# State space outputs through DRAM: the projection of a hybrid decoder step moved out of the chunk scan into three dense passes

## The chip, the cores and the metric

One Trainium2 chip, one core of it. The metric is the device time of one execution in microseconds (us), as the median of several runs. Five engines work beside each other: PE (TensorE, matmuls; its weight loads are listed as PEld), DVE (VectorE), ACT (ScalarE), POOL (GpSimd) and SP (SyncE, which here issues every DMA). Matmul results land in PSUM banks, everything else lies in SBUF or in DRAM.

## What is computed

One layer of a hybrid decoder step, for 1024 prompt tokens and 8 single-token samples that share the weights (1032 columns in all, D = 1024). A modulated RMSNorm feeds one input projection `h @ w_in`, whose columns are q, k, v of 12 attention heads, the state space streams z, xBC and dt, and two branch gates. Then, for each of 8 state space groups (256 channels each):

```
y   = scan(conv(xBC), dt) + d_skip * x         # chunks of 128 tokens, one state per head
y   = y * silu(z)
y   = y * rsqrt(mean(y*y over the group) + eps) * norm_g
```

and for the layer

```
merged = sigmoid(g_a) * (attn @ w_o_attn) + sigmoid(g_s) * (y @ w_o_ssd)     # y has 2048 channels
x      = x + g1 * (merged @ w_out)
x      = x + g2 * (relu(norm(x) @ w_up)**2 @ w_down)
```

All of it in float32 accuracy: each operand of a matmul is split into a rounded part and a remainder (hi, lo), and a product is three matmuls, hi·hi, hi·lo and lo·hi.

## The kernel before

**Layout.** Activations lie transposed: 128 channels on the partitions, the 1032 tokens along the row, in three column chunks of 384, 384 and 264 (`CH`).

**Dense jobs.** `Dense` (line 101) makes 128 output channels. It loads its weights through `load_raw` (SP), casts them on ACT (`whi`, line 97) and subtracts on POOL (`wlo`, line 98). Then, per column chunk, it accumulates 3 matmuls for each of 8 input tiles (lines 142 to 144) into one of three PSUM banks `mm` and calls an evacuation. A step is such a column chunk: 24 matmuls with 8 input tiles, 12 with 4, 6 with 2. `run` (line 181) loads the weights of the next job ahead, and after each step advances `clock` by one and lets the side work go on by `pace` items (`pump`, line 158).

**Side work.** Generators in `sides` yield between items. `rest(n)` makes one wait for n steps, so that the dense matmuls of those steps stand between two items on PE. The order on PE is that in which the program is written; on the other engines a planner orders the instructions. While `gated[0]` is set, a step whose activations find too few free `ck` buffers (19 of 384 columns and 10 of 264, counted in `live`) first drains side items two at a time (line 134).

**The scan stage.** The main jobs are z (2 jobs) and x/B/C (4 jobs, with the convolution in their evacuation, line 798) of each group. Beside them run, per group (`ssd_sides`, line 815): `chunks` (line 1002; 8 chunks, each `prep`, `state`, `out`; `prep` is called two chunks ahead), `decode` (line 824; the samples' states) and `finish_` (line 1034). `finish_` takes each column chunk through `sums` (product with the gate z on POOL, squares), `rstd` (a reciprocal root in ten small DVE instructions on 3 columns) and `norm` (three transposes on PE that spread the root, the scaling at line 969, hi on ACT, lo on POOL). Then it calls `project` (line 976):

```
for f in range(8):                       # 128 output channels each
    for ci, (t0, nt) in enumerate(CH):
        ps = ps_mm()
        for t in range(2):               # 2 tiles x 3 matmuls, lines 991 to 993
            ...
        V.tensor_tensor(sacc[f][:, t0:t0 + nt], ps[:, :nt], sacc[f][:, t0:t0 + nt], op=OP.add)   # 997
```

So each group adds its share of `y @ w_o_ssd` to eight accumulators in SBUF (`sacc`), 24 times 6 matmuls.

**After the scan.** Eight jobs for the attention gate (`ga_job`, line 1160), eight for the state space gate (`gs_job`, line 1166) with the merge of the three attention groups beside them (`merge`, line 1192), eight for the attention's output projection (`oa_job`, line 1243; only 2 input tiles, so 6 matmuls a step, and a chain of DVE, POOL, ACT and DVE behind each), then `w_out` (`wo_job`, line 1264), norm and MLP.

Of the kernel before, what the change touches and what calls it, by code (L numbers as in the profile page):

```python
# [19 lines left out]
NT = S + NB  # L20
# [20 lines left out]
def _trunk(ctx, tc, nc, I, O):  # L41
# [42 lines left out]
    def load_w(src, r0, kt, c0, n, side=False, into=None, raw=None):  # L84
# [3 lines left out]
        if into:  # L88
            hi, lo = into
        elif side:  # L90
            hi = wp.tile([128, 256], F32R, name="shi", tag="shi", bufs=2)
            lo = wp.tile([128, 256], F32R, name="slo", tag="slo", bufs=2)
# [8 lines left out]
    class Dense:  # L101

        def __init__(self, src, r0, c0, n, x, evac, pre=None, halo=0):
            self.a = (src, r0, c0, n, x, evac, pre)
            self.halo = halo
            self.units = self.raw = None

        def fetch(self, kt=4):
            if self.raw is None:
                src, r0, c0, n, x, *_ = self.a  # L110
                nk = self.nk = len(x[0]) if isinstance(x, tuple) else 8
# [101 lines left out]
    dsel = consts.tile([128, 16, 17], F32, name="dsel")  # L213

# [5 lines left out]
    ac_d = dram.tile([2, 32, 1024], F32, name="ac_d")  # L220

# [53 lines left out]
    def rstd_cols(sq, scale, eps, pool):  # L275

        ps = ps_()
        for i in range(3):
            T.matmul(ps[:, i:i + 1], sq[:, i * 128:(i + 1) * 128], ones, start=True, stop=True)
        r = pool.tile([128, 3, 3], F32, name="rstd", tag="rstd", bufs=2)  # L280
        V.tensor_scalar(r[:, 1], ps[:, :3], scale, eps, op0=OP.mult, op1=OP.add)
# [465 lines left out]
    sacc = []  # L747

    def acc_tiles():
        return [accp.tile([128, NT], F32, name="acc", tag="acc", bufs=8) for _ in range(8)]  # L750
# [64 lines left out]
    def ssd_sides(gi, tl):  # L815
# [8 lines left out]
        def decode():  # L824
# [13 lines left out]
            def load(bh):  # L838
# [37 lines left out]
        def load(c):  # L876
# [3 lines left out]
            ar = D_[c] = sd.tile([128, 4, 128], F32, name="ar", tag="ar", bufs=3)  # L880
            dma(ar, dap(ac_d, 4 * gi * 1024 + c * 128, [[0, 128], [1024, 4], [1, 128]]))

        def prep(c):
            ar = D_.pop(c)
            er = None
            if c:
                er = sd.tile([128, 2, 128], F32, name="er", tag="er", bufs=2)
# [59 lines left out]
        sq_, rs_, hi_, lo_ = {}, {}, {}, {}  # L947

        def sums(ci):
            nt = CH[ci][1]  # L950
# [603 lines left out]
```

## Time and profile before

| | |
|---|---|
| runs, us | 2492.43 median; 2486.13 to 2492.50 (3 runs) |
| the profiled execution, us | 2494.12; its span from first to last instruction 2492.3 |
| PE busy | 2357.0 us, 95% of the span, 15243 matmuls and transposes |
| DVE, ACT, POOL busy | 51%, 35%, 30% |
| TensorE clock granted, mean | 0.98 of full speed |
| DMA | 254.75 MB, 16 engines 35% busy |

Matmuls are pipelined, so "busy" covers small losses: how long matmuls take is read better from how many of them a stretch holds. A wait is listed with what ended it. In the listing of waits the columns are the total in us, the number of times and the longest.

### The profile page before, as it was taken

Reading aid. Unit: us, or ns where it says so; the run is one execution under the profiler, and the core shown is the slowest. Engines: PE = TensorE matmul, PEld = TensorE weight load, DVE = VectorE, ACT = ScalarE, POOL = GpSimd, SP = SyncE. Lnnn points to the kernel's source line nnn. Section 1 sums busy time; section 2 is a strip of 40 time slices with the busy share of each in tenths; the row PEclk is TensorE's granted clock in tenths of the full one; section 3 lists DMA queues with packets and bytes.
Section 4 is the critical chain, followed back from the end, with each engine's and each line's share of the span. In section 5 each row is a group of like instructions: output and inputs, shape, how many; then the busy total and the mean of one; then the engine's idle time right before and its main releaser. Section 6 shows DMA issues by size and latency. Waiting matters only on the chain.

```text
span 2492.3 us, 40904 instructions
## 1 busy us (share of the span) xinstructions
PE 2357.0 (95%) x15243; PEld 2240.5 (90%) x15243; DVE 1264.3 (51%) x3520; ACT 863.1 (35%) x2162; POOL 738.7 (30%) x702
## 2 busy tenths in 40 slices
PE   4999999999999999999999999989999999999998
PEld 2878898988999999989898999989999999999997
DVE  4443233577576768676767434345533333333336
ACT  4333333355543444434343312224321221221232
POOL 1011121244343434434343433343222222222230
PEclk7999999999999999999999999999999999999999
DMA  8254433343433333332333223122544544411111
GB/s 282 82 184 142 149 88 87 102 117 82 103 83 88 90 81 104 78 102 71 100 75 96 61 60 76 51 88 58 174 135 136 174 139 144 146 45 51 55 40 69
DMA packets 332481, 254.75 MB, mean 102 GB/s; under 512 B 21510, under 2 KB 323129, under 8 KB 326506
## 3 DMA queue, kind: packets, MB, share of 16 engines
q1 hardware_dynamic: 332282, 252.14, 34.9%
q8 instruction: 120, 1.97, 0.3%
q14 instruction: 79, 0.65, 0.1%
HBM read 224.50 MB, written 71.81 MB: 119 GB/s over the span
## 4 chain that ended last, share of the span: by engine, by line
PE 53%; DVE 10%; DMA 7%; POOL 3%; issue 3%; ACT 3%; SPq 0%; DVEq 0%; POOLq 0%; ACTq 0%
PE mm L142 16%; PE mm L143 16%; PE mm L144 16%; DMA ar<-ac_d 3%; DVE ck L798 2%; POOL wlo L98 1%; DMA hst<-state_ssm 1%; DVE hst L863 1%; DVE acc L997 1%; DMA bc<-bc_d 1%; ACT ar L907 1%; DMA ssm_sample<-hst 1%; PE ps L935 1%; PE mm L991 1%; PE mm L993 1%
## 5 line engine op out<-in xcount | busy, mean ns | idle before, releaser
L142 PE MATMUL mm<-hh,whi 128*128 128x384 f32 (+3 forms) x2808 | 917.8, 327 | 4.5 <-DVE ck L798 4.5
L144 PE MATMUL mm<-hh,wlo 128*128 128x384 f32 (+3 forms) x2808 | 900.4, 321 | 0.0
L143 PE MATMUL mm<-hl,whi 128*128 128x384 f32 (+3 forms) x2808 | 899.7, 320 | 0.1
L98 POOL TENSOR_TENSOR wlo<-wraw,whi 128x512 fp32r<-128x512 f32 (+1 forms) x300 | 388.4, 1300 | 973.0 <-ACT whi L97 930.9
L142 PEld LDWEIGHTS mm<-hh,whi 128*128 128x128 f32 x2808 | 532.8, 190 | 10.7 <-issue 6.7
L143 PEld LDWEIGHTS mm<-hl,whi 128*128 128x128 f32 x2808 | 532.1, 190 | 0.7 <-DVE hl L1324 0.3
L144 PEld LDWEIGHTS mm<-hh,wlo 128*128 128x128 f32 x2808 | 531.1, 189 | 0.0
L97 ACT CAST whi<-wraw 128x512 fp32r<-128x512 f32 (+1 forms) x300 | 181.8, 612 | 384.5 <-PE mm L143 325.4
L1257 DVE SCALAR_TENSOR_TENSOR acc<-mm,mod,acc 128x384 f32<-128x384 f32 (+1 forms) x216 | 123.6, 573 | 235.3 <-PE mm L144 234.4
L143 PE MATMUL mm<-dl,whi 128*128 128x384 f32 (+1 forms) x696 | 223.3, 321 | 0.0
L144 PE MATMUL mm<-dh,wlo 128*128 128x384 f32 (+1 forms) x696 | 222.3, 319 | 0.0
L142 PE MATMUL mm<-dh,whi 128*128 128x384 f32 (+1 forms) x696 | 222.3, 319 | 0.0
L798 DVE SCALAR_TENSOR_TENSOR ck<-mm,cwT,ck 128x384 f32<-128x384 f32 (+4 forms) x288 | 163.1, 568 | 69.5 <-ACT ck L794 65.8
L1344 DVE TENSOR_TENSOR r<-r 128x384 f32<-128x384 f32 (+1 forms) x96 | 70.0, 729 | 186.3 <-ACT r L1343 186.3
L991 PE MATMUL mm<-ck,shi 128*128 128x384 f32 (+1 forms) x384 | 129.8, 338 | 22.3 <-DVE acc L997 18.4
L910 POOL TENSOR_TENSOR ar<-ar,cb 128x512 f32<-128x512 f32 x64 | 83.2, 1300 | 163.1 <-DVE cb L905 129.6
L142 PEld LDWEIGHTS mm<-dh,whi 128*128 128x128 f32 x696 | 131.1, 188 | 0.0
L143 PEld LDWEIGHTS mm<-dl,whi 128*128 128x128 f32 x696 | 130.9, 188 | 0.0
L144 PEld LDWEIGHTS mm<-dh,wlo 128*128 128x128 f32 x696 | 130.8, 188 | 0.0
L993 PE MATMUL mm<-ck,slo 128*128 128x384 f32 (+1 forms) x384 | 124.5, 324 | 0.5 <-POOL slo L98 0.4
L992 PE MATMUL mm<-ck,shi 128*128 128x384 f32 (+1 forms) x384 | 124.0, 323 | 0.4 <-POOL ck L974 0.4
L907 ACT ACTIVATE ar<-ar,acs 128x128 f32<-128x128 f32 x256 | 85.4, 391 | 109.3 <-DMA ar<-ac_d 109.3
(334 smaller groups left out, 3404.0 us busy)
## 6 DMA issues: line engine op xcount, KB each, us to landing
wraw<-w_in SPq DMA_DIRECT2D x164, 256.0 KB
kv_g_sample<-cache_kv_g SPq DMA_DIRECT2D x144, 256.0 KB
wada<-w_ada SPq DMA_DIRECT2D x24, 1024.0 KB
ar<-ac_d SPq DMA_DIRECT2D x64, 256.0 KB
wraw<-w_up SPq DMA_DIRECT2D x64, 256.0 KB
wraw<-w_down SPq DMA_DIRECT2D x58, 256.0 KB
hst<-state_ssm SPq DMA_DIRECT2D x64, 128.0 KB
bc<-bc_d SPq DMA_DIRECT2D x32, 256.0 KB
```

Source lines behind the costliest of these rows:

```text
L97: A.copy(hi, raw)
L98: P.tensor_tensor(lo, raw, hi, op=OP.subtract)
L142: T.matmul(ps[:n, :m], wh, a, start=(k == 0), stop=False)
L143: T.matmul(ps[:n, :m], wh, b, start=False, stop=False)
L144: T.matmul(ps[:n, :m], wl, a, start=False, stop=(k == nk - 1))
L798: V.scalar_tensor_tensor(acc[:, o:n], ps[:, x0 + o - d:x0 + n - d], w[k], acc[:, o:n], op0=OP.mult, op1=OP.add)
L907: A.activation(ar[:, h, :], ar[:, h, :], AF.Relu, bias=acs[:, c, 4 * gi + h:4 * gi + h + 1], scale=-1.0)
L910: P.tensor_tensor(ar, ar, cb[:, None, :].to_broadcast([128, 4, 128]), op=OP.mult)
L991: T.matmul(ps[:, :nt], hi[:, t, :], a, start=(t == 0), stop=False)
L992: T.matmul(ps[:, :nt], hi[:, t, :], b, start=False, stop=False)
L993: T.matmul(ps[:, :nt], lo[:, t, :], a, start=False, stop=(t == 1))
L1257: V.scalar_tensor_tensor(x[:, t0:t0 + n], ps[:, :n], gate[:, 0:1], x[:, t0:t0 + n], op0=OP.mult, op1=OP.add)
```

## The change

The projection leaves the scan. In the scan a group's gated output `y` is written to DRAM (`y_d`) without its norm, and only the sums of squares are kept (`ysum`). The sixteen gate jobs write the tanh of their results to DRAM (`tg_d`): five stand between the x and B/C jobs of the groups 1 to 5, six behind the last z job, five after the scan. After the scan `yprep` reads `y` back in four quarters of four tiles, normalises it and splits it (hi on ACT, lo now on DVE). `y @ w_o_ssd` becomes three passes of eight dense jobs, with 4, 4 and 8 input tiles; the jobs of the last pass alternate with those of the attention's output projection. The scan's buffers get deeper, and `prep` runs three chunks ahead.

```diff
+    ysum = consts.tile([128, 8, 9], F32, name="ysum")
+    y_d = dram.tile([16, 128, NT], F32, name="y_d")
+    tg_d = dram.tile([16, 128, NT], F32, name="tg_d")
...
-                    hst = sd.tile([128, 2, 128], F32, name="hst", tag="hst", bufs=3)
+                    hst = sd.tile([128, 2, 128], F32, name="hst", tag="hst", bufs=4)
...
-            ar = D_[c] = sd.tile([128, 4, 128], F32, name="ar", tag="ar", bufs=3)
+            ar = D_[c] = sd.tile([128, 4, 128], F32, name="ar", tag="ar", bufs=5)
...
-            xd = sd.tile([128, 4, 64], F32, name="xd", tag="xd", bufs=2)
-            xw = sd.tile([128, 4, 64], F32, name="xw", tag="xw", bufs=2)
-            bt = sd.tile([128, 128], F32, name="bt", tag="bt", bufs=2)
-            cb = sd.tile([128, 128], F32, name="cb", tag="cb", bufs=1)
+            xd = sd.tile([128, 4, 64], F32, name="xd", tag="xd", bufs=4)
+            xw = sd.tile([128, 4, 64], F32, name="xw", tag="xw", bufs=4)
+            bt = sd.tile([128, 128], F32, name="bt", tag="bt", bufs=4)
+            cb = sd.tile([128, 128], F32, name="cb", tag="cb", bufs=2)
...
+        def gate(ci):
+            t0, nt = CH[ci]
             sq = sq_[ci] = [sd.tile([128, 384], F32, name="sq", tag="sq", bufs=2) for _ in range(2)]
             for t in range(2):
                 P.tensor_tensor(X[t][ci][:, :nt], X[t][ci][:, :nt], Z[t][ci][:, :nt], op=OP.mult)
+                dma(y_d[2 * gi + t, :, t0:t0 + nt], X[t][ci][:, :nt])
                 A.activation(sq[t][:, :nt], X[t][ci][:, :nt], AF.Square)
...
-        def rstd(ci):
...
-        def norm(ci):
...
-        def project():
...
+            live[ci // 2] -= 4
+
+        def sums(ci):
+            V.tensor_copy(ysum[:, gi, 3 * ci:3 * ci + 3], col_sums(sq_[ci][0]))
...
             prep(0)
             yield
             prep(1)
-            yield from rest(2)
+            yield from rest(1)
+            prep(2)
+            yield from rest(1)
             for c in range(8):
                 state(c)
                 yield
                 out(c)
-                if c + 2 < 8:
-                    prep(c + 2)
-                load(c + 3)
+                if c + 3 < 8:
+                    prep(c + 3)
+                load(c + 4)
...
+                gate(ci)
+                yield from rest(2)
                 sums(ci)
-                yield from rest(2)
-                rstd(ci)
-                yield from rest(2)
-                norm(ci)
                 yield
-            yield from project()
...
+    def gate_job(i, f, pool, bufs):
+        def ev(ci, t0, nt, ps):
+            t = pool.tile([128, 384], F32, name="tg", tag="tg", bufs=bufs)
+            A.activation(t[:, :nt], ps[:, :nt], AF.Tanh, scale=0.5)
+            dma(tg_d[8 * i + f, :, t0:t0 + nt], t[:, :nt])
+        return Dense(w_in, 0, (GA_C, GS_C)[i] + f * 128, 128, h_, ev)
...
-            main = main + x_jobs(gi + 1, tls[gi + 1])
+            xj = x_jobs(gi + 1, tls[gi + 1])
+            if gi < 5:
+                xj.insert(2, gate_job(*gates.pop(0), sa, 3))
+            main = main + xj
         sides.extend(ssd_sides(gi, tls[gi]))
+    main = main + [gate_job(*gates.pop(0), sa, 3) for _ in range(6)]
     run(main, pace=4.0)
...
+    def yprep(q, tiles):
...
+        r = mg.tile([128, 3, 18], F32, name="yr", tag="yr", bufs=2)
+        V.tensor_scalar(r[:, 1], ysum[:, 2 * q:2 * q + 2, :].rearrange("p g c -> p (g c)"), 1.0 / 256, 4 * EPS,
+                        op0=OP.mult, op1=OP.add)
+        rsqrt_cols(r[:, 0], r[:, 1], r[:, 2])
+        parts = [(g, ci) for ci in range(3) for g in range(2)]
...
+                    y = tg()
+                    dma(y[:, :nt], y_d[4 * q + 2 * g + t, :, t0:t0 + nt])
...
+        load(0)
+        load(1)
+        yield from rest(1)
+        for i, (g, ci) in enumerate(parts):
+            nt = CH[ci][1]
+            ps = ps_()
+            for k in range(3):
+                c = 9 * g + 3 * ci + k
+                T.transpose(ps[:, k * 128:(k + 1) * 128], r[:, 0, c:c + 1].to_broadcast([128, 128]), ident)
+            for t in range(2):
+                y = st[i][t]
+                c = R_SG + 4 * q + 2 * g + t
+                V.scalar_tensor_tensor(y, y, vecT[:, c:c + 1], ps[:, :nt], op0=OP.mult, op1=OP.mult)
+                hi, lo = (x[2 * g + t][ci] for x in yx[q])
+                A.copy(hi, y)
+                V.tensor_tensor(lo, y, hi, op=OP.subtract)
+            load(i + 2)
+            yield from rest(1)
...
+    def os_job(q, f):
+        def ev(ci, t0, nt, ps):
+            if q == 0:
+                A.copy(sacc[f][ci], ps[:, :nt])
+            elif q == 1:
+                V.tensor_tensor(sacc[f][ci], ps[:, :nt], sacc[f][ci], op=OP.add)
+            else:
+                t = ts[f, ci] = tg()[:, :nt]
+                g = tg()[:, :nt]
+                dma(g, tg_d[8 + f, :, t0:t0 + nt])
+                V.tensor_tensor(t, ps[:, :nt], sacc[f][ci], op=OP.add)
+                V.scalar_tensor_tensor(t, g, 1.0, t, op0=OP.add, op1=OP.mult)
...
+    preps = [yprep(q, x) for q, x in enumerate((yt_tiles, hl_tiles, ac_tiles, yt_tiles))]
+    mgs = merge()
+    sides.extend([preps[0], mgs])
+    os_ = [[os_job(q, f) for f in range(8)] for q in range(3)]
+    run([gate_job(*g, gt, GTB) for g in gates], after=os_[0][0], pace=3.0)
+    finish([preps[0], mgs])
...
+    sides.extend(preps[1:3])
+    run(os_[0], after=os_[1][0], pace=1.0)
+    finish([preps[1]])
+    sides.append(preps[3])
+    run(os_[1], after=os_[2][0], pace=1.0)
+    finish(preps[2:])
...
+    run([j for f in range(8) for j in (os_[2][f], oa_job(f))], after=wo[0])
     x1 = acc_tiles()
+    for f in range(8):
+        dma(x1[f], xT_d[f])
...
+    for f in range(4, 8):
+        wo[f].load(into=[tuple(wx.tile([128, 512], F32R, name="wx", tag="wx", bufs=16) for _ in range(2))
+                         for _ in range(2)])
```

`tg()` gives a tile of 384 columns from nine buffers, `ps_()` one of five PSUM banks. The side items of `yprep` and of the merge advance by at most one each per step.

## Rows read from the trace of the kernel before

**Rows 1.** Busy time per stretch: us, each engine's busy us (instructions), clock, DMA share, GB/s

```profile
core 0: us, PE busy (x) PEld busy (x) DVE busy (x) ACT busy (x) POOL busy (x), PEclk, DMA share, GB/s
1800.00:2300.00 500.00, 500.00 (x3183) 500.00 (x3182) 168.88 (x358) 108.19 (x211) 112.16 (x87) 1.00 0.38 120
...
490.00:1460.00 970.00, 923.28 (x6073) 877.28 (x6072) 658.27 (x1945) 418.86 (x1086) 385.89 (x381) 0.99 0.34 89
```

**Rows 2.** The same view for the eight project blocks: first, last, sum

```profile
611.30:638.00 26.70, 25.18 (x147) 24.70 (x146) 15.62 (x67) 18.50 (x53) 8.08 (x10) 0.92 0.56 158
...
1445.30:1473.60 28.30, 24.53 (x148) 22.94 (x147) 19.69 (x56) 4.56 (x13) 13.19 (x19) 1.00 0.36 95
sum 223.50, PE 200.28 PEld 185.51 DVE 178.90 ACT 82.75 POOL 71.48; mean PE 25.03 PEld 23.19 DVE 22.36 ACT 10.34 POOL 8.94
```

**Rows 3.** Instructions of line 991: durations ns, first and last start; waits until

```profile
L991 PE MATMUL mm<-ck,shi x384: 279/334/882, 611.3 to 1473.2; 128*128 128x384 f32 x128, 128*128 128x264 f32 x64
...
  DVE acc L997: 30.5, 42
```

**Rows 4.** Waits of PE over the whole span

```profile
PE mm L142 <- DVE ck L1247: 10.3, 6, 2.4
PE ps L966 <- DVE rstd L233: 8.0, 6, 4.0
...
PE ps L935 <- POOL ar L910: 6.7, 4, 2.2
```

**Rows 5.** Waits of PE from 490 to 1460 us

```profile
PE ps L931 <- DVE state L922: 4.5, 4, 1.8
```

**Rows 6.** Instructions that use the merged attention (tile ath): the projection's first matmuls

```profile
L142 PE MATMUL mm<-ath,whi x48: 282/338/687, 1605.3 to 1642.5; 128*128 128x384 f32 x32, 128*128 128x264 f32 x16
```

**Rows 7.** Busy time per stretch: group 2's scan beside z jobs, beside x jobs, group 0

```profile
757.00:787.00 30.00, 30.00 (x212) 28.30 (x211) 12.88 (x34) 9.99 (x26) 10.96 (x11) 1.00 0.31 78
787.00:833.00 46.00, 43.02 (x278) 41.59 (x277) 37.43 (x96) 24.07 (x59) 20.19 (x19) 0.96 0.27 68
...
523.00:548.00 25.00, 19.70 (x127) 17.14 (x127) 22.24 (x64) 12.63 (x33) 11.53 (x11) 0.92 0.50 134
```

**Rows 8.** DVE instructions by shape, 490 to 1660 us: busy us, mean ns, idle before

```profile
L997 DVE TENSOR_TENSOR acc<-mm,acc 128x384 f32<-128x384 f32 x112 | 61.5, 550 | 6.3 <-PE mm L993 6.2
...
L969 DVE SCALAR_TENSOR_TENSOR ck<-ck,vecT,ps 128x384 f32<-128x384 f32 x32 | 18.8, 605 | 8.4 <-PE ps L966 8.4
...
L969 DVE SCALAR_TENSOR_TENSOR ck<-ck,vecT,ps 128x264 f32<-128x264 f32 x16 | 7.7, 486 | 18.3 <-PE ps L966 18.3
```

**Rows 9.** DVE instructions by shape, 1475 to 1660 us

```profile
L1250 DVE TENSOR_TENSOR hl<-acc,hh 128x384 fp32r<-128x384 f32 x16 | 12.9, 809 | 7.0 <-ACT hh L1249 7.0
...
L1171 DVE SCALAR_TENSOR_TENSOR acc<-ck,acc 128x264 f32<-128x264 f32 x8 | 7.2, 904 | 14.3 <-ACT ck L1169 14.3
L1250 DVE TENSOR_TENSOR hl<-acc,hh 128x264 fp32r<-128x264 f32 x8 | 5.5, 687 | 7.2 <-ACT hh L1249 7.1
...
L1219 DVE TENSOR_TENSOR m<-m 128x256 f32<-128x256 f32 x5 | 4.1, 819 | 5.3 <-POOL m L1218 5.3
```

**Rows 10.** ACT instructions by shape, 490 to 1660 us

```profile
L1249 ACT CAST hh<-acc 128x384 fp32r<-128x384 f32 x16 | 8.2, 514 | 16.4 <-POOL acc L1248 16.4
```

**Rows 11.** POOL instructions by shape, 490 to 1460 us

```profile
L98 POOL TENSOR_TENSOR wlo<-wraw,whi 128x512 fp32r<-128x512 f32 x98 | 130.5, 1338 | 93.7 <-ACT whi L97 87.2 <-PE mm L143 5.6 <-PE mm L144 0.8
```

**Rows 12.** Busy time per stretch: gate jobs with the merge, the attention's projection

```profile
1475.00:1600.00 125.00, 120.67 (x766) 119.44 (x765) 35.83 (x100) 29.10 (x75) 36.19 (x38) 1.00 0.22 54
1605.00:1650.00 45.00, 34.59 (x188) 32.41 (x188) 29.44 (x50) 15.52 (x34) 35.00 (x34) 0.92 0.43 132
```

**Rows 13.** Waits of the DMA queue (SP), 490 to 1800 us

```profile
SPq L81 <- POOL wlo L98: 452.0, 130, 17.2
...
SPq L889 <- DVE xd L900: 62.4, 13, 8.1
```

**Rows 14.** Instructions of line 81 on SP, 490 to 1660 us: ns to issue one

```profile
L81 SPq DMA_DIRECT2D wraw<-w_o_ssd x64: 367/373/458, 596.2 to 1459.7; - x64
```

More of the change, by code (lines that the diff above doesn't have):

```diff
@@ L82, in load_raw, with load_w @@
         return raw
-    def load_w(src, r0, kt, c0, n, side=False, into=None, raw=None):
+    def load_w(src, r0, kt, c0, n, into=None, raw=None):
         if raw is None:
@@ L273, in steps, with col_sums @@
             yield
-    def rstd_cols(sq, scale, eps, pool):
+    def col_sums(sq):
         ps = ps_()
@@ L746, in _trunk, with acc_tiles @@
     sd = None
-    sacc = []
-    def acc_tiles():
-        return [accp.tile([128, NT], F32, name="acc", tag="acc", bufs=8) for _ in range(8)]
+    def acc_tiles(dt=F32):
+        return [accp.tile([128, NT], dt, name="acc", tag="acc", bufs=8) for _ in range(8)]
     def z_jobs(gi, tl):
@@ L1004, in chunks @@
                 yield 'wait'
-            for c in range(3):
+            for c in range(4):
                 load(c)
@@ L1144, in _trunk @@
     sd = sd_cm.__enter__()
-    accp = ctx.enter_context(tc.tile_pool(name="accp", bufs=1, side="right"))
-    sacc.extend(acc_tiles())
+    def gate_job(i, f, pool, bufs):
[4 more added lines that the diff above has]
+        return Dense(w_in, 0, (GA_C, GS_C)[i] + f * 128, 128, h_, ev)
+    gates = [(i, f) for i in range(2) for f in range(8)]
     main = zj0
@@ L1275, in wo_job @@
         return Dense(w_out, 0, f * 128, 128, lambda: g_, ev)
-    def xT_side():
-        for f in range(8):
-            while len(oa_done) <= f:
-                yield 'wait'
-            yield from rest(1)
-            dma(x1[f], xT_d[f])
-            yield
-    sides.append(merge())
-    oa = [oa_job(f) for f in range(8)]
-    mgs = list(sides)[-1]
-    run(gs, pace=3.0)
-    finish([mgs])
-    g_ = h_tiles()
-    x1 = acc_tiles()
-    oa_done = []
-    wo = [wo_job(f) for f in range(8)]
-    sides.append(xT_side())
-    run(oa, pace=0.7, after=wo[0])
-    drain()
+    ts = {}
+    preps = [yprep(q, x) for q, x in enumerate((yt_tiles, hl_tiles, ac_tiles, yt_tiles))]
[4 more added lines that the diff above has]
+    finish([preps[0], mgs])
+    mm_cm.__exit__(None, None, None)
+    accp = ctx.enter_context(tc.tile_pool(name="accp", bufs=1, side="right"))
+    sacc = [[hp_.tile([128, nt], F32, name="sacc", tag=f"hh{ci}", bufs=8) for ci, (_, nt) in enumerate(CH)]
+            for _ in range(8)]
+    sides.extend(preps[1:3])
[4 more added lines that the diff above has]
+    finish(preps[2:])
+    g_ = tuple([[] for _ in range(8)] for _ in range(2))
+    wo = [wo_job(f) for f in range(8)]
+    run([j for f in range(8) for j in (os_[2][f], oa_job(f))], after=wo[0])
+    x1 = acc_tiles()
+    for f in range(8):
+        dma(x1[f], xT_d[f])
+    yt_cm.__exit__(None, None, None)
+    mg_cm.__exit__(None, None, None)
+    wx_cm = tc.tile_pool(name="wx", bufs=1)
+    wx = wx_cm.__enter__()
     n2_cm = tc.tile_pool(name="n2", bufs=1, side="right")
```

143 lines of the change are left out of this document (61 added, 82 removed).

## The prediction

> **What bounds the kernel now.** I read the busy times by stretch first. In the MLP PE works without a gap: 500 us hold 3183 matmuls, so one costs 500/3183 = 0.1571 us on the mean of the three column chunks, at full clock [rows 1]. That is the price of a dense matmul when nothing disturbs it. In the scan PE is named busy for 923 of 970 us, DVE for 658 [rows 1], and still no single engine is full: PE executes in written order, so it loses time wherever a side item is not ready. Next I looked for the stretches that hold too few matmuls. The eight blocks of `project` are such: each has 144 matmuls with nothing dense between them, and together they last 223.5 us [rows 2], where 8 × 144 × 0.1571 = 181.0 us would do. The reason stands in the waits of line 991: the PSUM bank is not free because line 997, the addition to `sacc`, has not run [rows 3]. A step there has only 6 matmuls (0.94 us) per addition of 0.55 us [rows 8], and DVE does the samples' states in the same stretch; it is busy for 178.9 of the 223.5 us [rows 2]. Then I read the waits of PE over the whole span [rows 4]: the reciprocal root ahead of `norm` (8.0 us), the decay matrix of `prep` from POOL (6.7 us) and the attention's projection (10.3 us), which also has 6 matmuls a step and a chain over four engines behind each.
>
> **The change part by part.** The matmuls stay the same in number: 1152 for `w_o_ssd` before, 8 × 3 × (12 + 12 + 24) = 1152 after; 72 transposes for the root before, 4 × 18 after. So PE's own work is not shortened, and all that can be won is lost time.
>
> *Removed.* (1) Dense passes give 12 or 24 matmuls per evacuation, 1.9 or 3.8 us against 0.55, or 2 × 0.55 in the third: 223.5 − 181.0 = **42.5 us**. (2) The attention's projection runs from 1605.3 to its last step at 1642.5 us [rows 6]: 37.2 us for 23 steps, whose 138 matmuls need 21.7; **15.5 us**. Between the jobs of the third pass, each 72 × 0.1571 = 11.3 us, its chain has room. (3) The root leaves the scan, **8.0 us**. (4) `prep` one chunk earlier gives POOL a further step of about 4 us, and the longest such wait is 2.2 us: **6.7 us** [rows 4]. Sum 72.7.
>
> *Added: yprep.* A tile of 384 columns costs DVE 0.605 to scale and 0.809 to subtract, one of 264 columns 0.486 and 0.687 [rows 8, 9]; a part (two tiles) 2.83 or 2.35 us, a quarter 4 × 2.83 + 2 × 2.35 = 16.0 us. Nothing reads these subtractions at once, but PE stands behind the scalings, since each part's transposes need one of five PSUM banks. In the first pass two quarters are due together, two parts per step of 12 × 0.1571 = 1.88 us. The twelfth part can only be transposed when the seventh has been scaled: 3.8 us (two steps) + 7 × 2.83 = 23.6, while PE without waits is there after 7 × 1.88 = 13.2. I take **10.4 us**. Bounds: 0, if the planner scales all parts ahead of the subtractions; 18 us if DVE also waits for the cast of 0.514 us on ACT [rows 10] in each tile (a part is then 3.9 us). In the second pass one quarter is due, and DVE has 2.83 + 0.55 per step, against 1.88, for six steps: 9 us behind, of which three banks `mm` cover some 6; **4 us**, bounds 0 and 12. With the last five gate jobs the first quarter stands beside the merge. Of the 35.8 us of DVE there before [rows 12], some 16 were line 1171 (16 × 0.552 us and 8 × 0.904 [rows 9]); the other 20 belong to five of nine merge items (line 1219 ran five times in it [rows 9]), so 4 us each. Per step that is 2.83 + 4 = 6.8 us against 3.8, for six steps 18 us behind, of which the three buffers of the merge cover about three steps; **5 us**, bounds 0 and 13.
>
> One rule speaks against moving the subtraction from POOL to DVE. The 0.809 us [rows 9] were measured while POOL was busy for 35.0 of 45 us [rows 12], so the disturbance by POOL is in them, and I add nothing. The Trainium skill ("SBUF — State Buffer", section "Who interferes with whom") says that a DVE instruction with two SBUF inputs and a GpSimd instruction that reads SBUF exclude each other, the later one waiting for the whole of the other. By that rule the eight `wlo` casts of the first pass, 1.338 us each [rows 11], could push DVE back by up to 10.7 us more, and the sum would come out that much later.
>
> *Added: DMA.* `y` and the gates make 4 × 8.45 MB (16 tiles of 128 × 1032 × 4 bytes, each written and read), 33.8 MB. At 120 GB/s for a share of 0.38 [rows 1] full use is about 316 GB/s (an estimate), so 107 us of all engines, spread over 1100 us in which a third of them is used. 192 issues at 0.37 us [rows 14] are 71 us of SP; its main wait is for raw weight buffers, 452 us [rows 13], so it has the room. What SP is moved past: each `y` store waits for POOL's product and each gate store for ACT's tanh, and the weight loads written behind them stand still meanwhile. The nearest such wait of the queue is 62.4 us in 13 times, 4.8 each [rows 13]; a job lasts 11.3 us and its weights are asked for a job ahead, so it is hidden. Cost 0, up to 4.8 us for every third of the 24 pairs of stores if a second wait comes on top (38 us).
>
> *Added: x1 and w_out.* The eight loads of x, 4.2 MB, can start only when the third pass has read the tiles that lay there; they take 4.2/0.316 = 13.4 us, beside `w_out`'s weights. The first evacuation comes 6.6 us later (2.8 us of attention steps, 3.8 of the first job). **3 us**, bounds 0 and 14.
>
> *Added: the scan without its project blocks.* In each block DVE did some 11 us of work besides its 24 additions (178.9/8 less 16 × 0.55 + 8 × 0.42). That goes beside z and x jobs. Beside z jobs DVE has room: 12.9 of 30 us busy; beside x jobs it is at 37.4 of 46 [rows 7], but 24 roots and scalings go from there. **4 us**, bounds −10 (the waits of the first group [rows 5] and their clock go too, thanks to deeper buffers) and 35.
>
> *Sum:* added 10.4 + 4 + 5 + 3 + 4 = 26.4. The profiled execution took 2494.1 (span 2492.3); 2494.1 − 72.7 + 26.4 = 2447.8. The median is 1.7 lower: **2446 us**.
>
> **Rivals.**
> *Little is given back.* The planner spreads yprep, and the deeper buffers end the first group's waits: 72.7 + 8 off, 2494.1 − 80.7 + 6 − 1.7 = 2418. For it: DVE is a third full after the scan [rows 1, 12]. Chance 0.15.
> *The preparation becomes the bound.* The three places of yprep and the entry to `w_out` at their upper bounds, 18 + 12 + 13 + 14 + 4 = 61: 2481. For it: DVE waits for ACT's cast behind most of line 1250 [rows 9]; against: the planner has other work to put in. 0.09.
> *The queue takes it back.* SP's stores hold up weights at the worst bound, 38 us beside the 26: 2484 or a little more, so no change. Against: 452 us of slack [rows 13]. 0.06.
> *Slower: the scan loses its cover.* From 523 to 548 us, with no project block in between, PE is busy for 19.7 of 25 us at clock 0.92 [rows 7], DVE for 22.2; it waits for line 922 [rows 5]. If the 11 us of DVE work that each block hid come onto PE's path in all eight groups, 88 us, the time is 2446 + 84 = 2530. It decides when the loss exceeds (72.7 − 22.4)/8 = 6.3 us per group. Against: the room beside z jobs [rows 7]. 0.05.
>
> **How the numbers follow.** The forecast has the remaining 0.65. Its own range is 2428 to 2466. The range for 8 in 10 reaches from 2416 (the better case) to 2482 (the preparation); outside stand the queue, the slower case and what is better still, some 0.18. A measurement of this kernel can tell about 0.3%, 7.5 us, from no change. Faster than 2485: forecast, better case and the preparation, 0.89; within: the queue, 0.06; slower: 0.05.
>
> **What would show it.** Right: the blocks of 6 matmuls are gone; no wait for lines 997, 233 and 1247 of before is left in PE's list; the three passes hold near 1/0.1571 matmuls per us except in the first seven steps of the first pass, where PE waits some 10 us for the scalings; each scan group shrinks by about 29 us, less the 11 of a gate job. Wrong: waits of PE for the state addition or the convolution in every group; PE waiting for casts whose weights landed late behind a store; or passes that run without a wait.

## The result: slower, where a gain was forecast

The changed kernel takes **2521.0 us** (median of 4 runs, 2507.2 to 2525.7), the kernel before 2490.0 (4 runs beside them, 2486.1 to 2492.5): ratio 1.0106, 95% interval 1.0086 to 1.0125. The ratio with its interval is the better measure: the two medians alone give 1.0125, so a difference taken between medians can be off by some 5 us. The forecast was 2446, its range 2416 to 2482. The profiled execution took 2519.6 us, its span is 2517.8.

The page's first row, and PE's waits over the whole span of the changed kernel (us in total, times, longest us), which answer to [rows 4, 5]. In the changed kernel line 926 is the state addition, 935 the matmul that reads the state of the chunk before, 920 the matmul that makes a state, 867 the update of a sample's state, 911 the first pass of the scalar engine over a decay tile `ar`.

```profile
PE 2366.4 (94%) x15243; PEld 2255.6 (90%) x15243; DVE 1200.8 (48%) x3252; ACT 867.0 (34%) x2126; POOL 682.8 (27%) x618
```
```profile
PE ps L935 <- DVE state L926: 30.2, 11, 5.4
...
PE mm L140 <- DVE tg L1287: 14.8, 8, 2.5
PE ps L935 <- ACT ar L913: 13.0, 6, 3.9
...
PE ps L935 <- ACT ar L911: 6.9, 6, 2.0
PE mm L140 <- DVE ysum L966: 6.0, 6, 1.0
```

The waits that were to go are gone: none for the project blocks' additions, the scan's reciprocal root, or the attention's projection of before. In their place PE waits for the state addition, 30.2 us where [rows 5] had 4.5, for the decay tiles, and in pass 3 eight times for line 1287, the attention's gate product.

Busy time by stretch of the changed kernel (us, each engine's busy us and instructions, granted clock, DMA share, GB/s): passes 1 to 3, then the scan, which answers to the second row of [rows 1].

```profile
1441.00:1494.00 53.00, 50.05 (x329) 49.18 (x329) 26.53 (x59) 25.27 (x56) 11.57 (x9) 1.00 0.53 160
1494.00:1541.00 47.00, 47.00 (x307) 46.83 (x306) 23.29 (x47) 10.67 (x21) 9.77 (x8) 1.00 0.18 53
1541.00:1672.00 131.00, 116.15 (x727) 114.70 (x726) 54.19 (x94) 24.07 (x46) 49.25 (x47) 1.00 0.37 116
490.00:1382.00 892.00, 830.85 (x5414) 791.88 (x5414) 528.33 (x1539) 389.72 (x987) 312.45 (x289) 0.96 0.42 109
```

Passes 1 and 2 run as dense work should. Pass 3 loses some 15 us, and the scan's mean clock is 0.96 where [rows 1] had 0.99.

From the first matmul of a state to the last, the scan took 891.8 us before and 804.5 after. By the prediction's own terms it should take 891.8 − 195.2 (seven of the eight blocks lie between, 223.5 − 28.3 [rows 2]) − 8.0 − 6.7 + 56.5 (five gate jobs of 11.3) + 4 = 742. It is 62 too long, and since the 4 are in the sum, the scan's own term came out at 66. Pass 3 with the attention's projection lasts 128.0 to its last job's matmuls; eight pairs of 14.1 (90 matmuls) need 113. These two excesses, 62 and 15, and 5.6 us in the first 510 us, where both kernels are the same, are 83; the span exceeds the forecast by 72, so 11 less must lie elsewhere (a remainder, not measured by itself).

One group shows what happened. Instructions of two lines in group 2 (durations ns min/median/max, first and last start): first before, where line 916 makes the states and line 863 updates the samples, then after.

```profile
L916 PE MATMUL ps<-xw,bt x16: 377/378/462, 726.3 to 797.0; 128*128 128x256 f32 x16
...
L863 DVE SCALAR_TENSOR_TENSOR hst<-hst,dsel,tmp x16: 341/345/1125, 732.5 to 755.3; 128x128 f32<-128x128 f32 x16
```
```profile
L920 PE MATMUL ps<-xw,bt x16: 377/378/463, 733.9 to 788.0; 128*128 128x256 f32 x16
...
L867 DVE SCALAR_TENSOR_TENSOR hst<-hst,dsel,tmp x16: 337/350/1389, 740.7 to 770.1; 128x128 f32<-128x128 f32 x16
```

The samples' update follows 6 to 7 us behind the first state in both. In that time before, no further state was made: in the stretch from 732 to 756 us line 916 has no instruction at all, because PE was in the project block (727.9 to 756.9). After, ten of the sixteen matmuls of line 920 lie between 740 and 771 us, beside the z jobs, whose last evacuation starts at 762.7. The chunks' chain now runs through the samples' update.

What such a meeting looks like, on DVE, then on ACT (start us, us, instruction, and in brackets the idle time before it and what ended it):

```profile
638.01 0.16 DVE L863 TENSOR_TENSOR dx<-ck,dsel 128x2 f32<-128x2 f32 x1
641.18 0.64 DVE L867 SCALAR_TENSOR_TENSOR hst<-hst,dsel,tmp 128x128 f32<-128x128 f32 x2 [3.01 <-ACT tmp L866]
641.74 0.42 DVE L926 TENSOR_TENSOR state<-ps,state 128x256 f32<-128x256 f32 x1
```
```profile
638.91 1.28 ACT L911 ACTIVATE ar<-ar,acs 128x128 f32<-128x128 f32 x4 [4.41 <-DMA ar<-ac_d]
640.22 0.63 ACT L913 ACTIVATE ar<-ar 128x512 f32<-128x512 f32 x1
640.76 0.68 ACT L866 ACTIVATE tmp<-bc,dx 128x128 f32<-128x128 f32 x2
```

ACT stands 4.4 us for a decay tile; the samples' product (line 866) is queued behind it; DVE stands 3.0 us for that product, and the state addition is queued behind the samples' update. PE waits 4.6 us for the addition. In these rows each engine takes up the next instruction only behind the late one, so one late load passes through three engines. The load itself stands on SP behind two stores of the samples' states:

```profile
626.73 4.47 SPq L871 DMA_DIRECT2D ssm_sample<-hst  x2
...
632.31 0.46 SPq L885 DMA_DIRECT2D ar<-ac_d  x1
```

### The profile page after: what moved, and what is told of

Read it like the earlier page. It is cut to its first block, busy times and chain, and to the rows that moved or that the text cites. A ratio compares the mean times of both kernels' runs of the same rounds, so it can differ in the third digit from the quotient of the medians.

```text
span 2517.8 us, 40894 instructions
## 1 busy us (share of the span) xinstructions
PE 2366.4 (94%) x15243; PEld 2255.6 (90%) x15243; DVE 1200.8 (48%) x3252; ACT 867.0 (34%) x2126; POOL 682.8 (27%) x618
## 4 chain that ended last, share of the span: by engine, by line
PE 57%; DMA 9%; DVE 6%; ACT 3%; issue 3%; POOL 2%; SPq 1%; DVEq 0%; ACTq 0%; POOLq 0%
PE mm L140 18%; PE mm L141 18%; PE mm L142 18%; DMA ar<-ac_d 7%; ACT ar L911 2%; DMA tg<-tg_d 1%; DVE ck L802 1%; POOL wlo L95 1%; POOL ck L957 1%; PE ps L939 1%; PE ps L935 0%; DVE hst L867 0%; POOL ar L914 0%; ACT ck L798 0%; DMA ssm_sample<-hst 0%
## 5 line engine op out<-in xcount | busy, mean ns | idle before, releaser
L95 POOL TENSOR_TENSOR wlo<-wraw,whi 128x512 fp32r<-128x512 f32 (+1 forms) x332 | 424.9, 1285 | 1176.0 <-ACT whi L94 1116.6
L140 PEld LDWEIGHTS mm<-hh,whi 128*128 128x128 f32 x2808 | 538.3, 192 | 17.3 <-issue 16.4
L141 PEld LDWEIGHTS mm<-hl,whi 128*128 128x128 f32 x2808 | 537.9, 192 | 0.5 <-DVE hl L1373 0.3
L94 ACT CAST whi<-wraw 128x512 fp32r<-128x512 f32 (+1 forms) x332 | 201.9, 613 | 490.3 <-PE mm L141 416.7
L1392 ACT ACTIVATE r<-mm 128x384 f32<-128x384 f32 (+1 forms) x96 | 43.8, 456 | 153.5 <-PE mm L142 152.9
L867 DVE SCALAR_TENSOR_TENSOR hst<-hst,dsel,tmp 128x128 f32<-128x128 f32 x128 | 60.9, 488 | 68.0 <-ACT tmp L866 67.5
L935 PEld LDWEIGHTS ps<-ck,state 128*128 128x128 f32 x224 | 33.4, 202 | 63.3 <-ACT tmp L866 27.7
## 6 DMA issues: line engine op xcount, KB each, us to landing
hst<-state_ssm SPq DMA_DIRECT2D x64, 128.0 KB
```

Source lines behind the costliest of these rows:

```text
L94: A.copy(hi, raw)
L95: P.tensor_tensor(lo, raw, hi, op=OP.subtract)
L140: T.matmul(ps[:n, :m], wh, a, start=(k == 0), stop=False)
L141: T.matmul(ps[:n, :m], wh, b, start=False, stop=False)
L867: V.scalar_tensor_tensor(hst[:, i, :], hst[:, i, :], ds[:, 8 + 2 * bh + i:9 + 2 * bh + i], tmp, op0=OP.mult, op1=OP.add)
L1392: A.activation(r[:, :nt], ps[:, :nt], AF.Relu)
```

## The experiments

**Buffers and look-ahead as before** (the change's edits to `bufs` and to `chunks` undone):

```diff
-            ar = D_[c] = sd.tile([128, 4, 128], F32, name="ar", tag="ar", bufs=5)
+            ar = D_[c] = sd.tile([128, 4, 128], F32, name="ar", tag="ar", bufs=3)
...
-                if c + 3 < 8:
-                    prep(c + 3)
+                if c + 2 < 8:
+                    prep(c + 2)
```

> The changed kernel (2521.0) with the buffers and the look-ahead of the kernel before: three ar tiles, two of xd, xw, bt and er, one cb, three hst, chunks prepared two ahead. Theory A (the scan pays because nothing lies between a chunk's state and the next chunk any more, whatever the buffers): 2515 to 2540, the same or a little worse. Theory B (the deeper buffers let the planner put work of later chunks and of the samples ahead of the state addition on the vector and scalar engines): 2450 to 2490, with the waits for the state addition (30.2 us on line 926 in the changed kernel) under 10.

2505.6 us, ratio to before 1.0074 (1.0052 to 1.0096): 15 us better, and the state waits are 36.5 us in 28 times. So the depth costs something, but the wait is there without it; neither theory's time was met.

**The state one chunk earlier:**

```diff
+            state(0)
             for c in range(8):
-                state(c)
+                if c < 7:
+                    state(c + 1)
                 yield
                 out(c)
```

> The changed kernel with each chunk's state computed one chunk earlier, so that the output of chunk c finds the state of chunk c-1 a whole chunk old; four state tiles in place of three. Nothing else moves. Theory A (the state addition comes late on the vector engine by a few us, seven times a group, and TensorE waits for it and then runs at half clock): the 30.2 us of waits on line 926 go to under 8, with the half-clock stretches behind them, and the time falls by 30 to 60, to 2460 to 2490. Theory C (the waits are of the scalar engine for the decay tile's load, which come late in any order): TensorE waits for ar in place of the state, and the time stays over 2505.

2488.7 us, ratio 0.9999 (0.9988 to 1.001): 32 us back (27 by the ratios), the scan 771.8, at the upper end of what theory A gave. What is left are mostly waits for `xw` (27.0 us in 8 times) and for a PSUM bank that a late state addition holds (13.8 in 10).

**The samples' states left out**, in the changed kernel and in the one before:

```diff
-            load(0)
-            yield from rest(2)
-            for bh in range(4):
+            for bh in range(0):
```

> The changed kernel without the loop over the samples' states (their loads, update, outputs and stores are left out, so the samples' rows of the scan lack the state term). Theory A (the samples' update collides with the chunks' chain on the vector and scalar engines, now that no projection block gives it a stretch of its own): the lost time of the scan falls by 40 to 70, to 2450 to 2480. Theory D (the collisions are with the convolution's evacuations and weight casts, not the samples): a fall of under 20, 2501 to 2521.

> The kernel before (2490.0) without the same loop over the samples' states. Theory A: the samples' update lay under the projection blocks, where TensorE needed nothing of the state's chain, so little is gained: 2475 to 2490. Theory D, and any theory in which the samples cost the same in both kernels: a fall as large as that of the changed kernel without the loop.

After: 2438.0 us, ratio 0.9798 (0.9783 to 0.9812), the scan 721.0. Before: 2453.6, ratio 0.9862 (0.9847 to 0.9877). The samples cost 83 us after and 37 before (77 and 34 by the ratios); without them the change gains 15.6 us. In the changed kernel that is more than the 40 to 70 of theory A. For the kernel before neither theory was met: the samples were not nearly free there, as theory A had it, and the fall is not as large as after, as theory D had it. In the scan of the changed kernel without samples PE waits for no state and no decay tile; its waits, and its stretch from the first state to the last:

```profile
PE mm L140 <- DVE ysum L964: 4.6, 5, 1.0
PE mm L140 <- DVE ck L802: 3.6, 4, 1.3
```
```profile
509.60:1230.60 721.00, 712.83 (x4873) 687.04 (x4873) 391.60 (x943) 320.89 (x789) 284.77 (x262) 1.00 0.33 86
```

That accounts for the 83: with the samples PE waits 57.8 us in this stretch at a mean clock of 0.96, without them 8.2 us at 1.00. So 50 us are waits, and up to 32 (0.04 of 804.5 us, an estimate) are the lower clock. ACT still stands 95.8 us for decay tiles without the samples, and 111.6 with them:

```profile
ACT ar L909 <- DMA ar<-ac_d: 95.8, 30, 5.2
```
```profile
ACT ar L911 <- DMA ar<-ac_d: 111.6, 43, 5.1
```

So late loads alone hold up nothing on PE in that run; together with the samples they do. The kernel before shows where most of its 37 us lay: the eight project blocks without samples, the sum of their windows beside the sum of [rows 2], and PE's wait for the blocks' additions (line 995 there):

```profile
sum 196.20, PE 187.82 PEld 183.30 DVE 100.59 ACT 49.28 POOL 70.17; mean PE 23.48 PEld 22.91 DVE 12.57 ACT 6.16 POOL 8.77
```
```profile
PE mm L989 <- DVE acc L995: 2.1, 2, 1.2
```

The blocks shrink from 223.5 to 196.2 us. Of the 42.5 us that I had put down to six matmuls per addition, 27 were the samples' work.

The next three each take one link out of the chain. **The product on DVE** (`V.tensor_scalar` for `A.mul`), **the new stores on ACT's queue** (those of `y`, shown below, and those of the gates), and **decay tiles and gate tanh loaded from ACT's queue**:

```diff
-                        A.mul(tmp, bc[:, 0, i, :], dx[:, i:i + 1])
+                        V.tensor_scalar(tmp, bc[:, 0, i, :], dx[:, i:i + 1], None, op0=OP.mult)
```

> The changed kernel (2521.0) with the samples' product tmp (128 products of 128x128) computed on the vector engine in place of the scalar engine. The samples' whole loop cost 83 us in the changed kernel and 37 in the kernel before. Theory A (the vector engine stands 67.5 us in the scan for this product, which lies on the scalar engine behind the decay tiles' wait for their load, and the state addition is queued behind it): the wait goes, and the time falls by 30 to 55, to 2466 to 2491, though the vector engine has some 35 us more to do. Theory E (the cost is the samples' work itself on a vector engine that has to do it ahead of the state addition): no fall, 2515 to 2540.

2515.9 us, ratio 1.0105 (1.0083 to 1.0126), as theory E had it. The wait for ACT is gone by construction, and PE's for the state grew to 50.8 us in 25 times. DVE has 31 us more to do in this run, so it does not tell how much the wait for `tmp` cost; but taking that wait out is not enough, and the samples' work in front of the addition delays it too.

```diff
-                dma(y_d[2 * gi + t, :, t0:t0 + nt], X[t][ci][:, :nt])
                 A.activation(sq[t][:, :nt], X[t][ci][:, :nt], AF.Square)
+                nc.scalar.dma_start(y_d[2 * gi + t, :, t0:t0 + nt], X[t][ci][:, :nt])
```

> The changed kernel with the stores that the change added to the scan (gated outputs to y_d, gate tanh to tg_d) issued by the scalar engine's queue, each right behind a scalar instruction that needs the same data, in place of SP's queue. Theory B (these stores hold SP's queue 83.6 and 30.2 us while they wait for their data, and make the decay tiles' loads late, for which the scalar engine waits 113 us in all): the scalar engine's wait for ar falls below 60 and the time by 25 to 50, to 2470 to 2496. Theory A (the stores are not the cause; the scalar engine waited 109 us for ar in the kernel before too): within 10 us of 2521.

2502.6 us, ratio 1.0041 (1.0023 to 1.0059); ACT's wait for `ar` fell from 111.6 to 84.7 in the scan, which is 787.5. PE's own waits for decay tiles (13.0 and 6.9 us) are gone from its list, while those for the state are 39.2. Between the two theories: the stores, costed at nothing, do cost something like 18 us (16 by the ratios).

```diff
-            dma(ar, dap(ac_d, 4 * gi * 1024 + c * 128, [[0, 128], [1024, 4], [1, 128]]))
+            nc.scalar.dma_start(ar, dap(ac_d, 4 * gi * 1024 + c * 128, [[0, 128], [1024, 4], [1, 128]]))
```

> The changed kernel with the decay tiles' loads in the scan, and the gate loads in the third pass, issued by the scalar engine's queue. In the scan, theory C (the late load of ar is the first cause: no lateness, no wait for tmp behind it): the scalar engine's wait for ar falls from 113 to under 40 and the scan's stretch from the first state to the last from 804 to 760 to 780. Against it: the scan stays over 795. In the third pass, if the gate loads are late because they stand behind weight loads in SP's queue, the eight waits of about 1.9 us for line 1287 go, and the stretch of pass 3 with the attention's projection shrinks from 128 to 110 to 116; if the vector engine's own order makes them, it stays. Time 2460 to 2485 if both hold.

2495.7 us, ratio 1.0023 (1.0013 to 1.0032), outside what was expected. The scan gave 15 us (789.2), pass 3 10 (117.7, with 7 lost behind it to a late last gate). ACT's wait for `ar` fell only to 81.1, so the loads stayed late and this run does not decide theory C. The run without samples speaks against it: ACT stood 95.8 us for loads as late, and PE waited for no state.

**The kernel before without its projection**, with shallow buffers, no new store and the root in its place:

```diff
             yield from rest(1)
-            for f in range(8):
-                fetch(f + 1)
...
+            if gi == 0:
+                for f in range(8):
+                    V.memset(sacc[f], 0.0)
             live[0] -= 8
```

> The kernel before (2490.0) without the projection inside the scan: its weights, matmuls and additions are left out and the sums are zero; the normalisation stays. Full speed of its matmuls is 181 us. Theory A, in the strict form (without the blocks, the samples' update hits the chunks' chain in any kernel, with the old shallow buffers too): the lost time that the samples cause goes from 37 to 60 or more, so 2490 - 181 - 11 for the blocks' own loss, + 25 or more, is 2323 or more. If the lost time stays what it was: about 2298. If it goes with the blocks, as the prediction had it: 2266 to 2280.

2325.2 us, ratio 0.9338 (0.9318 to 0.9358): taking out 181 us of matmuls, and the blocks' own loss, gave 167. It meets the strict form of theory A (2323 or more), though only just. Lines 916 and 863 in its group 2, and its largest wait in the scan:

```profile
L916 PE MATMUL ps<-xw,bt x16: 377/378/454, 710.7 to 758.4; 128*128 128x256 f32 x16
...
L863 DVE SCALAR_TENSOR_TENSOR hst<-hst,dsel,tmp x16: 335/348/1416, 716.0 to 743.9; 128x128 f32<-128x128 f32 x16
```
```profile
PE ps L931 <- DVE state L922: 33.5, 22, 3.3
```

The samples' update lies on the chunks as in the changed kernel, and that kernel's wait appears in the old one as soon as the block is gone. That is the cover, shown without any other part of the change.

Then edits together. **State early, decay tiles from ACT's queue, gate tanh loaded one job ahead** (15 tiles in place of 9); **the same with the samples' update split** into steps of one tile; **the split alone**; and **the state early in the kernel before** (the edit above). The gates' and the split's edits:

```diff
+            if job.units is None:
+                for ci, (t0, nt) in enumerate(CH):
+                    gs[k, ci] = tg()[:, :nt]
+                    dma(gs[k, ci], tg_d[k, :, t0:t0 + nt])
+            load(*a, **b)
```
```diff
-                yield from rest(2)
+                    yield from rest(1)
             tl['dec'] = 1
```

> The changed kernel with three edits: each chunk's state one chunk earlier (alone 2488.7), the decay tiles' loads from the scalar engine's queue (with late gate loads 2495.7, of which the scan gave some 15 and pass 3 about 10), and the gate tanh of a job of pass 3 loaded when the job's weights are loaded, one job ahead, with 15 tiles in place of 9. If the two scan edits take away different parts of the wait, 2521 - 32 - 15 - 17 = 2457; if both only shorten the same lateness, the scan is as with the first alone and the time is 2521 - 32 - 17 = 2472. Pass 3 with the attention's projection: 110 to 113 us in place of 128 to 132.

> As the run before, and the samples' update in steps of one tile with one main chunk after each, in place of two tiles and then two chunks. If the vector engine's bursts of the samples' work (two tiles at a time, eight operations) are what the state addition still waits behind, the remaining waits fall once more: 10 to 20 below the run before. If the sum of the samples' work decides and not its bursts: the same within 5.

> The changed kernel (2521.0) with only the samples' update split, one tile per step. Bursts decide: 2485 to 2505. Sum of work decides: within 7 of 2521.

2479.8 (0.9952, 0.9935 to 0.997), 2488.9 (0.9985, 0.9971 to 0.9998) and 2515.0 (1.0097, 1.008 to 1.0115). The first is slower than either sum that was expected. Loading gates a job ahead brings pass 3 to 113.2 us, its floor. Alone the split gains 6 us, within the spread of the changed kernel's runs; on top of the others it costs 9, and the moved loads don't add to the early state: the scan is 781.4, where the early state alone had 771.8.

> The kernel before (2490.0) with each chunk's state one chunk earlier, as in the run that brought the changed kernel from 2521 to 2488.7. Theory A (in the kernel before the projection blocks stood between the chunks and hid the late state): TensorE waited 4.5 us in all for the state, so the gain is under 10: 2480 to 2490. If the late state cost both kernels the same: about 2458.

2518.7, ratio 1.0113 (1.0096 to 1.0131): slower, which no theory had. There the chunks are prepared only two ahead, and PE waits for `xw`, which the preparation has not made; the waits for the additions in the blocks stay (18.4 us before):

```profile
PE ps L916 <- DVE xw L903: 35.0, 19, 4.8
PE mm L991 <- DVE acc L997: 21.6, 28, 3.0
```

So the early state helps the changed kernel and harms the one before. Look-ahead and cover differ between them, and no run parts the two.

What was open: is it the overlap in time, or the samples' work at all? **Samples held back in program order** until the group's eight chunks are written, alone, with the early state and gates, and with more room (`CKB` 12 for 10); and early state and gates without that:

```diff
             load(0)
+            while tl['c'] < 8:
+                yield 'wait'
             yield from rest(2)
```

> The changed kernel (2521.0) with the samples' update of a group held back until the group's eight chunks are done; nothing is left out. Theory A in its precise form (the samples' update costs TensorE only because it lies beside the chunks' chain in time; the stretch in which the main matmuls run and no chunk is under way hides it, as the projection blocks did in part): most of the 83 us that the samples cost come back, 2450 to 2480, and the waits for the state addition fall from 30 to under 8. Theory E (the work has to be done anyway and delays whatever is beside it, then the convolution's evacuations and the next group's first chunks): over 2505.

> The changed kernel with each chunk's state one chunk earlier and the gate tanh of pass 3 loaded one job ahead; the decay tiles' loads stay on SP's queue. The run with these loads moved too was 2479.8, with a scan 9 us longer than with the state edit alone. If the moved loads cost those 9 us once the state is early: 2468 to 2474. If the scan differs by chance of the order: about 2480.

> Both of the runs before together: samples after the chunks, state one chunk earlier, gate tanh one job ahead. Theory A: with no samples beside the chain the early state has little left to hide, so about 2521 - 60 - 17 = 2445 to 2460 and no waits for the state worth 5 us. Theory E: 2475 or more.

> As the run before, with 12 in place of 10 tiles for the last chunk of the group's convolution outputs, since the samples' delay keeps these tiles longer. If the delay makes the next group's convolution wait for a tile: 5 to 15 below the run before. If not: the same within 4.

2517.0 (1.0097, 1.0076 to 1.0119), 2471.8 (0.9925, 0.9911 to 0.994), 2492.6 (1.0006, 0.9996 to 1.0017) and 2488.1 (0.9987, 0.9977 to 0.9998). The second confirms that the moved loads cost some 9 us once the state is early (scan 772.8 without them). The three that hold the samples back tell nothing against theory A, because the start of the samples' update did not move: it comes 6 us behind the group's first state in each of them (group 2). Why the two with the early state are some 20 us slower than without the holding back stays open. Group 2 of the first of them:

```profile
L922 PE MATMUL ps<-xw,bt x16: 377/378/462, 730.7 to 784.6; 128*128 128x256 f32 x16
...
L869 DVE SCALAR_TENSOR_TENSOR hst<-hst,dsel,tmp x16: 332/351/1384, 736.8 to 766.3; 128x128 f32<-128x128 f32 x16
```

Writing the work later moved nothing on DVE: the planner put it back beside the chunks. A **data dependency** moves it: the samples' first product takes a factor of exactly 1 that is made from the last state. These runs keep the holding back and also have the 12 tiles (`CKB`), which were worth 4.5 us between the last two runs above and were not tried alone with the dependency.

```diff
+                        V.tensor_scalar(one, S_[7][:, :1], 0.0, 1.0, op0=OP.mult, op1=OP.add)
-                    V.tensor_tensor(dx[:, :2], xcol, ds[:, 2 * bh:2 * bh + 2], op=OP.mult)
+                    V.scalar_tensor_tensor(dx[:, :2], xcol, one, ds[:, 2 * bh:2 * bh + 2], op0=OP.mult, op1=OP.mult)
```

> The run that held the samples' update back in program order did not move it: the planner, which orders every engine but TensorE, put it back beside chunks 1 to 5 (736.8 to 766.3 us in a group whose chunks ran 730.7 to 784.4). Here the samples' first product takes a factor of exactly 1 worked out from the state of chunk 7, so the update cannot start before the group's last state; 12 tiles for the last chunk's convolution outputs. No work is left out. Theory A (overlap in time with the chunks' chain): the waits for the state addition, 30.2 us and 22 chances in the changed kernel, fall under 8 and the time to 2445 to 2475. Theory E (the work has to be done somewhere and costs there as much): over 2500, with the waits on the convolution's evacuations or on the samples' tiles.

> As the run before, with each chunk's state one chunk earlier and the gate tanh of pass 3 loaded one job ahead (together 2471.8 without the samples moved). Theory A: pass 3 gives 15 to 17 us as before and the early state little, 2430 to 2460. Theory E: 2470 to 2500.

(The changed kernel's 30.2 us were 11 waits, as its list shows, not 22.)

**2468.7 us** (0.9904, 0.9885 to 0.9924) and **2457.7** (0.9867, 0.9847 to 0.9887). Group 2, and PE's waits in the scan, of the first:

```profile
L925 PE MATMUL ps<-xw,bt x16: 377/378/463, 714.3 to 755.8; 128*128 128x256 f32 x16
...
L872 DVE SCALAR_TENSOR_TENSOR hst<-hst,dsel,tmp x16: 342/352/839, 767.8 to 786.2; 128x128 f32<-128x128 f32 x16
```
```profile
PE mm L140 <- DVE ck L802: 27.3, 18, 5.1
...
PE ps L940 <- DVE state L931: 0.7, 1, 0.7
```

All the work is done, only later: the wait for the state falls from 30.2 to 0.7 us, the chunks take 41 us in place of 54, and the scan 750.8 at a mean clock of 0.99, 8 more than the 742.4 of the prediction's terms. Both numbers of theory A are met. So overlap in time is the cause of 52 of the 83 us (50 of 77 by the ratios), of which the tiles may have given a few. The remaining 31 lie, by PE's list, mostly in waits for the convolution (line 802, 27.3 us, where the run without samples had 3.6), among whose instructions the samples' update now stands on DVE. With the early state and gates the change beats the kernel before by 1.3%; of these two only the gates still gain (pass 3 from 134.0 to 113.2, of which 5 are lost again between the scan and pass 3), the early state has nothing left to hide (scan 749.4).

## Why the prediction was wrong

*The cause is the rival with chance 0.05*, "the scan loses its cover": 2530 forecast, 2521 measured, and its wait is the one named (the state addition). It was to decide above 6.3 us lost per group; the loss is 66/8 = 8.3. That the two times lie so close is partly luck: the rival put 88 us into the scan and nothing into pass 3, and the runs have 66 and 15.

*The step that failed* is the scan without its project blocks, 4 us with bounds −10 and 35: it measured 66. I asked only whether DVE had room by its busy share (12.9 of 30 us beside z jobs [rows 7]). It had: the samples' update did go beside the z jobs, and DVE was busy for 25.1 of the 31 us from 740 to 771 in group 2. But the chunks run there as well. What counts is where the samples' update lies in time, and what stands behind it in DVE's order. It starts 5 to 7 us behind the group's first state, with a block there or without one, and so it met the chunks as soon as the block was gone. The row that told this was read: group 0, with no block in it, PE 19.7 of 25 us busy at clock 0.92 [rows 7]. It was the only group in which the chunks ran without a block between them, that is, the changed kernel in small. PE's waits for the state from 523 to 548 us, and the samples' update of that group, in the kernel before:

```profile
PE ps L931 <- DVE state L922: 3.6, 3, 1.8
```
```profile
L863 DVE SCALAR_TENSOR_TENSOR hst<-hst,dsel,tmp x16: 336/352/1457, 515.0 to 559.3; 128x128 f32<-128x128 f32 x16
```

So 3.6 of the 4.5 us of [rows 5] lay in this one group, where the samples' update lay on the chunks. I put them down to shallow buffers, which the runs contradict: the wait is 30.2 us with deep buffers, and the shallow ones are 15 us the faster in the changed kernel.

*Removed, 72.7.* The four waits did go, but 27 of the 42.5 us of the first were the samples', whose work stayed in the kernel. It was counted as the price of six matmuls per addition because line 997 ended the waits [rows 3]; DVE's 178.9 busy us [rows 2] fall to 100.6 without samples.

*Attention's projection, 15.5.* Gone as such and back in pass 3, 15 us: line 1287 stands 24.8 us in 15 times for its gate load, which SP issues behind a weight load that waits for a free buffer first (87.3 us in 16 times in pass 3, line 81). The prediction had no term for it; it costed only the stores. One job of head start removes it.

*yprep, 10.4 + 4, and 5 beside the merge.* Oversized: PE waited 2.9 us for a scaling (line 1203), and pass 1 holds 329 instructions in 53 us, pass 2 runs full. DVE subtractions of passes 1 and 2 (line 1206: busy us, mean ns, idle before):

```profile
L1206 DVE TENSOR_TENSOR yt<-tg,yt 128x384 fp32r<-128x384 f32 x8 | 5.2, 669 | 0.1
L1206 DVE TENSOR_TENSOR yl<-tg,yl 128x384 fp32r<-128x384 f32 x8 | 5.0, 620 | 0.0
L1206 DVE TENSOR_TENSOR acc<-tg,acc 128x384 fp32r<-128x384 f32 x8 | 4.4, 547 | 0.0
```

They take 547 to 669 ns where 809 had been taken from a stretch with POOL busy for 35.0 of 45 us [rows 9, 12]; here POOL is busy for 11.6 of 53 and 9.8 of 47. That is the direction of the rule cited from the Trainium skill ("SBUF — State Buffer", section "Who interferes with whom"), but the further delay that it threatened, up to 10.7 us of PE's time, did not come: PE is idle for 3 of the 53 us of pass 1. No run changes POOL's work alone.

*DMA and SP at 0.* About 18 us by the run with the stores on another queue, inside the 38 of the bound. They are part of the 66, since that run's scan is 17 us shorter. The prediction looked for them in late weights; what the run shows is decay tiles that come earlier, so the 452 us of slack that SP has for weights [rows 13] did not cover them. How the 18 us divide is not shown.

*x1 and w_out, 3.* From the attention's last job to the MLP 148.9 us after, 149.7 before: nothing.

*Sums.* Three of the prediction's own steps do not come out as written: 178.9/8 less 16 × 0.55 + 8 × 0.42 is 10.2, not 11, which makes the 88 of the rival 82; 18 less three steps of 3.8 beside the merge is 7, not 5; and 13.4 less 6.6 for x1 is 7, where 3 were taken. Together they move the forecast by 6 us at most and decide nothing.

## What to carry over

Before a block of matmuls is moved out, look at what the other engines do during it: work that an engine must do anyway may be hidden there, and it may land on the next thing that waits for that engine. A stretch of the old kernel without the block, even one group, was here a better guide to this than busy shares. Where a planner orders the engines, as here, writing work later need not make it run later; a data dependency did.

## What was not expected of the hardware

How much TensorE's clock adds to a short wait. The changed kernel around the wait above, by stretch:

```profile
630.00:637.00 7.00, 7.00 (x55) 6.65 (x54) 6.52 (x24) 3.45 (x11) 1.91 (x2) 1.00 0.54 140
637.00:642.00 5.00, 0.74 (x5) 0.34 (x3) 1.92 (x11) 3.05 (x9) 0.00 (x0) 0.94 0.42 113
642.00:648.00 6.00, 5.70 (x25) 5.17 (x26) 6.00 (x18) 2.48 (x7) 4.45 (x5) 0.50 0.62 178
648.00:652.00 4.00, 4.00 (x24) 3.70 (x22) 4.00 (x6) 2.57 (x7) 2.80 (x3) 0.97 0.29 95
```

In the 6 us that follow 4.6 us of waiting the granted clock is 0.50, that is 1.2 in place of 2.4 GHz, so this wait costs some 3 us on top (an estimate, half of the 6). Over the scan the mean clock fell from 0.99 to 0.96, which is up to 36 us of 892 against 10 of 970 (estimates, 0.04 and 0.01 of the stretches).
